# Stationary weights for the gate, up, key and query products of a two-layer hybrid decoder trunk

## The chip, the cores and the metric

The kernel runs on one core of one Trainium2 chip. The metric is the device time of one execution in microseconds (us), read as the median of the executions shown; lower is better.

## The reference

Sequence of 256 rows, width 1024, all float32. Two layers; each is a feed-forward network (FFN), a token mixer, and a second FFN, with RMS norms ahead of and behind each of them. The mixer of layer 0 is a gated causal convolution, that of layer 1 is causal attention with 8 heads. So there are four FFNs, numbered 0 to 3, with the convolution between 0 and 1 and the attention between 2 and 3.

```python
def rms_norm(x, g):
    y = x * lax.rsqrt(jnp.mean(x * x, axis=-1, keepdims=True) + RMS_EPS)
    return y * g

def swiglu_ffn(h, w_gate_up, w_down):          # 1024 -> 2 x 2816 -> 1024
    gate, up = jnp.split(h @ w_gate_up, 2, axis=-1)
    return (jax.nn.silu(gate) * up) @ w_down

for layer in range(2):
    f = swiglu_ffn(rms_norm(x, ffn_norm_pre[layer, 0]), ffn_w_gate_up[layer, 0], ffn_w_down[layer, 0])
    x = x + 0.5 * rms_norm(f, ffn_norm_post[layer, 0])
    h = rms_norm(x, mix_norm_pre[layer])
    y = conformer_conv(h, ...) if layer == 0 else attention(h, ...)   # attention: q, k, v, scores, softmax, values, w_o
    x = x + rms_norm(y, mix_norm_post[layer])
    f = swiglu_ffn(rms_norm(x, ffn_norm_pre[layer, 1]), ffn_w_gate_up[layer, 1], ffn_w_down[layer, 1])
    x = x + 0.5 * rms_norm(f, ffn_norm_post[layer, 1])
```

## The kernel before, in words

**Three products for one.** Every large product is made in fp32r from values split in two parts: `hi` is the value cast to fp32r by ScalarE (ACT), `lo` is what is left, value minus `hi`, by VectorE (DVE). A product is then hi·hi + hi·lo + lo·hi, three matmuls into one PSUM bank (`mm3` at L189 to L193, `rows_product` at L277 to L284).

**Weights.** `plan()` writes out the order in which 320 weight pieces of 128x1024 (512 KB) are used. SP's queue loads them in that order into four `raw` buffers (L155); `split_piece` (L158 to L179) makes `whi` on ACT and `wlo` on DVE, scaled by the norm's gain, into nine pairs of buffers (`wspl`). `use` keeps the order ten pieces ahead. A `raw` buffer is free when it is split, a `wspl` pair when the last matmul that reads it is done. A gate and up unit of an FFN has four pieces (each two of the eight contraction slices `k`, with 256 columns of gate and 256 of up), each down row block one.

**Activations.** `xT` holds the transposed rows, hi and lo, as two tiles of 8 slices x 256 columns. `turn(tt)` (L249 to L261) makes them for the rows of half `tt` (0 or 1): eight 128x128 PE transposes into two banks, then ACT's copy (L265) and DVE's difference (L266).

**An FFN** (`ffn`, L295) runs over 11 units of 256 hidden columns. For each unit and each half of the rows `gate_up(i, tt)` makes 24 matmuls with a slice of `xT` stationary and 512 weight columns moving, so the bank holds rows by [gate | up]; ACT applies silu (L310) and DVE multiplies (L311), both scaled by `rstds[tt]`, the reciprocal root of the pre norm, because the rows in `xT` were not normalised: in mode `"ffn"`, `pre_norm` (L228) hands the raw residual rows `xs` to `turn` and computes the reciprocal root beside it. `turn_act(i)` (L313) transposes the unit's activation by four PE transposes (L319) and splits it (L322, L323); `down` multiplies it with the down weights into four banks of accumulators. The first `FLEAD` units (1 for FFN 0, else 2) run half 0 of all of them before half 1, so that `turn(1)` can come later.

**The end of an FFN.** The down products of half 1 for the last 7 row blocks (`DEFER`) are kept for the end: `COVERED` of them run ahead of the last pair of half 0, then `after(0)` (post norm, residual, next pre norm, on ACT, DVE and POOL) starts, and the others run under it; `turn(0)` of the next stage stands ahead of the last two. `after(1)` follows the last one.

**Attention.** `kq(h)` makes the transposed keys and queries of a head in one bank of 2 x 256 columns, with the weights stationary and a part of `xT` (256 columns) moving: 24 matmuls each. Evicting them takes four instructions (L617 to L620). Then scores, softmax, transposed probabilities, values and output rows, with `kq` of the next head between a head's softmax and its probabilities.

**Order and PSUM.** The framework's scheduler orders each engine's instructions ahead of time by a priority (program order, raised by `tc.high_priority`) and by its own estimate of when an operand is ready; at run time each engine works in that order. Of the eight banks four are accumulators (tag `acc`), two are `mm` (products) and two `tr` (transposes, scores, spectra, values).

Of the kernel before, what the change touches and what calls it, by code (L numbers as in the profile page):

```python
# [20 lines left out]
F32 = mybir.dt.float32  # L21
F32R = mybir.dt.float32r
AF = mybir.ActivationFunctionType
# [28 lines left out]
COVERED = 1  # L52
# [45 lines left out]
def trunk(ctx, tc, x, wpk, gains, gcol, pvec, dft, wdw, bvec, out):  # L98
# [33 lines left out]
    pw = ps.tile([P, T], F32, name="pw", tag="mm")  # L132
# [56 lines left out]
    def mm3(out_ap, wh, wl, xh, xl, start, stop):  # L189

        nc.tensor.matmul(out_ap, wh, xh, start=start, stop=False)  # L191
        nc.tensor.matmul(out_ap, wh, xl, start=False, stop=False)  # L192
        nc.tensor.matmul(out_ap, wl, xh, start=False, stop=stop)  # L193
# [11 lines left out]
    def sumsq(src):  # L205
        junk = t2.tile([P, 512], F32, name="junk", tag="junk", bufs=2)
# [19 lines left out]
    rstds = {}  # L226

    def pre_norm(tt, pre):  # L228


        if pre == "ffn":
            normed[tt] = xs[:, tt, :].rearrange("p (h n) -> p h n", h=2)
        s = [sumsq(xs[:, tt, h * 512:(h + 1) * 512]) for h in range(2)]
        r, last = rstd_of(s[0], s[1], 1.0 / D, RMS_EPS)
        if pre == "ffn":
            rstds[tt] = r
            return last
        t = t4.tile([P, 2, 512], F32, name="xg", tag="t4")
        for h in range(2):
            xsl = xs[:, tt, h * 512:(h + 1) * 512]  # L240
            if pre is None:
                last = nc.vector.tensor_scalar(t[:, h, :], xsl, r, None, op0=ALU.mult)
            else:
                last = nc.vector.scalar_tensor_tensor(t[:, h, :], xsl, r, gain_t[pre][h],
                                                      op0=ALU.mult, op1=ALU.mult)
        normed[tt] = t
        return last

    def turn(tt, between=()):  # L249

        xg = normed.pop(tt)
        for h in range(2):
            p = ps.tile([P, 4, P], F32, name="ptr", tag="tr")
# [31 lines left out]

    def rows_unit(p, w, tt):

        for k in range(KD):
# [3 lines left out]
            mm3(p, xh, xl, wh[:, c], wl[:, c], k == 0, k == KD - 1)  # L292


    def ffn(f, after, *gains_used):  # L295
# [4 lines left out]
        def gate_up(i, tt):  # L300
# [5 lines left out]
            p = ps.tile([P, 2, 2 * P], F32, name="pgu", tag="mm")  # L306
            rows_unit(p.rearrange("p a b -> p (a b)"), w, tt)
            with tc.high_priority(offset=400):
                s = t2.tile([P, 2 * P], F32, name="sg", tag="sg", bufs=2)
                nc.scalar.activation(s, p[:, 0, :], AF.Silu, scale=rstds[tt])  # L310
                nc.vector.scalar_tensor_tensor(a[:, tt, :], p[:, 1, :], rstds[tt], s, op0=ALU.mult, op1=ALU.mult)  # L311

        def turn_act(i):  # L313

            a = raws.pop(i)[1]
            pt = ps.tile([P, 2, T], F32, name="pta", tag="tr")
# [29 lines left out]
        for i in range(FLEAD[f]):  # L346
            gate_up(i, 0)
        turn(1)
        for i in range(FLEAD[f]):
            gate_up(i, 1)  # L350
            if i:
                turn_act(i - 1)
        for i in range(FLEAD[f], NP):
# [6 lines left out]
            gate_up(i, 0)  # L360
            turn_act(i - 1)
            gate_up(i, 1)
# [31 lines left out]
    def conv_constants():  # L394
# [8 lines left out]
        for j in range(2):  # L403
            for h in range(2):
                p = ps.tile([NB, 512], F32, name="psp", tag="tr")
# [32 lines left out]
    def conv(after):  # L438
# [9 lines left out]
        def in_unit(q, tt):  # L448
# [5 lines left out]
            p = ps.tile([P, 2, 256], F32, name="pag", tag="mm")  # L454
# [15 lines left out]
        def filter_(h, tt):  # L470

            cols = slice(h * 512, (h + 1) * 512)
            with tc.high_priority(offset=300):
                U = []
                for j in range(2):
                    p = ps.tile([NB, 512], F32, name="pU", tag="tr")
# [20 lines left out]
        def layer_norm(tt):  # L497

            y = yacc[tt]
            with tc.high_priority(offset=300):  # L500
# [13 lines left out]
                for h in range(2):  # L514
                    p = ps.tile([P, 4, P], F32, name="pz", tag="tr")
# [40 lines left out]
    def attention(after):  # L556
# [45 lines left out]
        def kq(h):  # L602
# [4 lines left out]
            p = ps.tile([P, 2, T], F32, name="pkq", tag="mm")  # L607
            for s, n in enumerate("kq"):
                for k in range(KD):
                    wh, wl = pieces_kq[h2][n][k // 4]  # L610
                    o = (k % 4) * 256 + hj * P
                    mm3(p[:, s, :], wh[:, o:o + P], wl[:, o:o + P], xT[0][:, k, :], xT[1][:, k, :],
                        k == 0, k == KD - 1)
            with tc.high_priority(offset=400):
                kh = t2.tile([P, 2, T], F32R, name="kT", tag="t2")
                qh = t2.tile([P, 2, T], F32R, name="qT", tag="t2")
                nc.scalar.copy(kh[:, 0, :], p[:, 0, :])  # L617
                nc.vector.tensor_sub(kh[:, 1, :], p[:, 0, :], kh[:, 0, :].bitcast(F32))
                nc.scalar.activation(qh[:, 0, :], p[:, 1, :], AF.Copy, scale=sc)
                nc.vector.scalar_tensor_tensor(qh[:, 1, :], p[:, 1, :], sc, qh[:, 0, :].bitcast(F32),  # L620
# [3 lines left out]
        def scores(h):  # L624
            kh, qh = hd[h]["kq"]
            pS = ps.tile([P, NT, T], F32, name="pS", tag="tr")
# [27 lines left out]
        def probs(h):  # L654

            s = hd[h]["s"]
            pp = ps.tile([P, 3, P], F32, name="pp", tag="tr")
# [12 lines left out]
        def values(h):  # L670
            a = pT[h % 2]
            po = ps.tile([P, T], F32, name="po", tag="tr")
# [42 lines left out]
    pre_norm(0, "ffn")  # L715
    last = turn(0, between=first[:1])
    with tc.issue_after(last[0].ins):
        pre_norm(1, "ffn")
# [3 lines left out]
    conv(chain("mpost0", False, "ffn"))  # L722
    ctx2.close()
    ffn(1, chain("fpost1", True, "ffn"), "fpost1")
    ffn(2, chain("fpost2", True, None), "fpost2")
    ctx2 = ExitStack()
    attention(chain("mpost1", False, "ffn"))
# [94 lines left out]
```

## Time and profile before

| | us |
|---|---|
| median of 3 runs (975.83 to 980.27) | 977.95 |
| the profiled execution | 977.37 |
| its span, first to last instruction | 975.6 |

The profiled execution lies 0.06% under the median, and 1.8 us of its time lie outside the span. TensorE's matmuls (PE in the rows) are pipelined: the duration in a row runs past the start of the next one, so what a matmul costs in a dense stretch is the distance between two starts. PEld is the load of the stationary operand. In rows, `pgu` is the bank of a gate and up unit, `pta` that of the transposed activation, `ptr` that of `turn`, `pkq` keys and queries, `acc` the accumulators. Stages by time: FFN 0 to 204, convolution to 299, FFN 1 to 487, FFN 2 to 675, attention to 783, FFN 3 to the end.

### The profile page before, as it was taken

The page shows a single profiled execution, that of the slowest core. Times are in us where ns is not written, and L with a number is a line of the kernel's source. Part 1 is how long each engine was busy: PE and PEld are TensorE (multiplying, and loading weights), DVE is VectorE, ACT ScalarE, POOL GpSimd, SP SyncE. Part 2 cuts the span into 40 slices and gives each one's busy share as a digit, 9 for nine tenths or more (in the row PEclk, how much of TensorE's full clock was granted, in tenths as well). Part 3 has the DMA queues.
Part 4 walks back from the last instruction along what each step waited for, and adds up shares of the span by engine and source line. Part 5 has one row for each costly group of instructions (what it writes and reads, how often), then busy time and mean ns, then how long its engine had stood idle before and what let it go on. Part 6 is the DMA issues. An engine that isn't in the chain of part 4 may idle for free.

```text
span 975.6 us, 12708 instructions
## 1 busy us (share of the span) xinstructions
PE 958.1 (98%) x4514; PEld 786.8 (81%) x4514; DVE 618.6 (63%) x1064; ACT 550.8 (56%) x1029; POOL 22.1 (2%) x46
## 2 busy tenths in 40 slices
PE   8999999999999999999999999999999999999997
PEld 6887888876668888888888888887899888888885
DVE  5874565586667755655776565648887776564643
ACT  7764554472446745544765555546776676464541
POOL 1000000010011000000000000000000000000000
PEclk9999999999999999999999999999999999999999
DMA  7866464554326764645466464636643457555531
GB/s 262 297 232 203 130 220 148 190 198 151 108 65 198 261 192 154 228 156 194 160 202 227 156 224 154 212 134 215 195 154 127 131 165 247 171 192 196 170 111 43
DMA packets 48783, 174.93 MB, mean 179 GB/s; under 512 B 5673, under 2 KB 5673, under 8 KB 48720
## 3 DMA queue, kind: packets, MB, share of 16 engines
q1 hardware_dynamic: 48720, 174.13, 53.6%
q8 instruction: 35, 0.57, 0.2%
q14 instruction: 28, 0.23, 0.1%
HBM read 173.06 MB, written 1.05 MB: 178 GB/s over the span
## 4 chain that ended last, share of the span: by engine, by line
PE 93%; DVE 3%; ACT 1%; issue 1%; DMA 1%; POOL 0%; SPq 0%; DVEq 0%; POOLq 0%; ACTq 0%
PE pgu L191 16%; PE pgu L192 16%; PE pgu L193 16%; PE acc L283 10%; PE acc L282 10%; PE acc L284 10%; PE pta L319 2%; PE pkq L193 1%; PE pkq L192 1%; PE pkq L191 1%; PE pag L193 1%; PE pag L192 1%; PE pag L191 1%; DMA xs<-in_x_dram 1%; PE ptr L255 1%
## 5 line engine op out<-in xcount | busy, mean ns | idle before, releaser
L172 DVE SCALAR_TENSOR_TENSOR wlo<-raw,gc,whi 128x512 fp32r<-128x512 f32 x352 | 247.2, 748 | 92.3 <-ACT whi L171 89.1
L171 ACT ACTIVATE whi<-raw,gc 128x512 fp32r<-128x512 f32 x352 | 234.0, 717 | 98.5 <-PE acc L283 61.5
L191 PE MATMUL pgu<-whi,xTh 128*128 128x512 f32 x704 | 278.9, 396 | 0.8 <-ACT xTh L265 0.7
L192 PE MATMUL pgu<-wlo,xTh 128*128 128x512 f32 x704 | 275.1, 391 | 0.1
L193 PE MATMUL pgu<-whi,xTl 128*128 128x512 f32 x704 | 274.5, 391 | 0.0
L178 DVE TENSOR_TENSOR wlo<-raw,whi 128x512 fp32r<-128x512 f32 x240 | 155.4, 686 | 19.2 <-ACT whi L176 18.3
L176 ACT CAST whi<-raw 128x512 fp32r<-128x512 f32 x240 | 137.1, 619 | 44.5 <-PE pag L193 18.1
L191 PEld LDWEIGHTS pgu<-whi,xTh 128*128 128x128 f32 x704 | 132.6, 188 | 28.8 <-ACT xTh L265 1.4
L193 PEld LDWEIGHTS pgu<-whi,xTl 128*128 128x128 f32 x704 | 132.6, 188 | 27.9
L192 PEld LDWEIGHTS pgu<-wlo,xTh 128*128 128x128 f32 x704 | 132.7, 189 | 27.0 <-DVE wlo L172 0.5
L311 DVE SCALAR_TENSOR_TENSOR ar<-pgu,rr,sg 128x256 f32<-128x256 f32 x88 | 42.4, 482 | 163.6 <-ACT sg L310 163.5
L310 ACT ACTIVATE sg<-pgu,rr 128x256 f32<-128x256 f32 x88 | 41.7, 474 | 178.7 <-PE pgu L193 178.3
L282 PE MATMUL acc<-whi,ahi 128*128 128x512 f32 x352 | 137.5, 391 | 0.0
L283 PE MATMUL acc<-whi,alo 128*128 128x512 f32 x352 | 137.4, 390 | 0.0
L284 PE MATMUL acc<-wlo,ahi 128*128 128x512 f32 x352 | 137.1, 390 | 0.0
L283 PEld LDWEIGHTS acc<-whi,alo 128*128 128x128 f32 x352 | 66.1, 188 | 14.2 <-DVE alo L323 0.8
L284 PEld LDWEIGHTS acc<-wlo,ahi 128*128 128x128 f32 x352 | 66.1, 188 | 13.6
L282 PEld LDWEIGHTS acc<-whi,ahi 128*128 128x128 f32 x352 | 66.1, 188 | 13.6
L172 DVE SCALAR_TENSOR_TENSOR wlo<-raw,pv,whi 128x256 fp32r<-128x256 f32 (+1 forms) x72 | 37.3, 568 | 2.8 <-ACT whi L171 2.7
L171 ACT ACTIVATE whi<-raw,pv 128x256 fp32r<-128x256 f32 (+1 forms) x72 | 36.3, 573 | 3.7 <-PE acc L283 1.6
L191 PE MATMUL pkq<-xTh,whi 128*128 128x256 f32 x128 | 36.5, 285 | 0.0
L192 PE MATMUL pkq<-xTl,whi 128*128 128x256 f32 x128 | 36.5, 285 | 0.0
(126 smaller groups left out, 876.1 us busy)
## 6 DMA issues: line engine op xcount, KB each, us to landing
raw<-in_wpk_dram SPq DMA_DIRECT2D x320, 512.0 KB, 4.4
gain<-in_gains_dram SPq DMA_DIRECT2D x7, 512.0 KB, 4.3
xs<-in_x_dram SPq DMA_DIRECT2D x4, 256.0 KB, 6.5
out_dram<-xs SPq DMA_DIRECT2D x4, 256.0 KB
dm<-in_dft_dram SPq DMA_DIRECT2D x1, 368.0 KB
taps<-in_wdw_dram SPq DMA_DIRECT2D x1, 124.0 KB
braw<-in_bvec_dram SPq DMA_DIRECT2D x6, 4.0 KB
ys<-in_bvec_dram SPq DMA_DIRECT2D x2, 2.0 KB
```

The lines of the kernel that those rows point to most:

```text
L171: nc.scalar.activation(hi[:, o:o + n], raw[:, o:o + n], AF.Copy, scale=g)
L172: nc.vector.scalar_tensor_tensor(lo[:, o:o + n], raw[:, o:o + n], g, hb[:, o:o + n], op0=ALU.mult, op1=ALU.subtract)
L176: nc.scalar.copy(hi[:, o:o + 512], raw[:, o:o + 512])
L178: eng.tensor_sub(lo[:, o:o + 512], raw[:, o:o + 512], hb[:, o:o + 512])
L191: nc.tensor.matmul(out_ap, wh, xh, start=start, stop=False)
L192: nc.tensor.matmul(out_ap, wh, xl, start=False, stop=False)
L193: nc.tensor.matmul(out_ap, wl, xh, start=False, stop=stop)
L282: nc.tensor.matmul(o, xh, wh[:, cols], start=first, stop=False)
L283: nc.tensor.matmul(o, xl, wh[:, cols], start=False, stop=False)
L284: nc.tensor.matmul(o, xh, wl[:, cols], start=False, stop=last)
L310: nc.scalar.activation(s, p[:, 0, :], AF.Silu, scale=rstds[tt])
L311: nc.vector.scalar_tensor_tensor(a[:, tt, :], p[:, 1, :], rstds[tt], s, op0=ALU.mult, op1=ALU.mult)
```

## The change

Four edits, with the constants `COVERED` from 1 to 2 and the new `FTURN` of 5.

1. `xT` becomes one tile of 8 slices x [hi 256 | lo 256], so that 512 moving columns take both parts. `both_parts` makes a product with a 128x128 block of weights stationary: per slice one matmul of `whi` with 512 columns (hi·hi lands in the left half of a bank, hi·lo in the right half) and one of `wlo` with the 256 hi columns, into the left half. `joined` sums the halves when the bank is read: ACT copies the right half to SBUF, DVE adds the left one.
2. Gate and up of all units from `FLEAD` on (10 in FFN 0, 9 in each of the others) are made that way, gate and up of 128 hidden columns each in a bank of its own. Their result is transposed already: `turn_act` stays for the first `FLEAD` units only. Keys and queries take the same form.
3. The mode `"ffn"` of the pre norm goes: the rows are multiplied by the reciprocal root before `turn`, at the start of every FFN, as it was done ahead of the attention. `gate_up_rows` (the first units) loses the scale.
4. The tags `mm` and `tr` become one of four banks. In FFN 0, `turn(1)` may issue only after the sixth slice (`FTURN`) of the first unit. `junk` has one buffer instead of two.

```diff
-COVERED = 1
+COVERED = 2
+FTURN = 5
...
     def pre_norm(tt, pre):
-        if pre == "ffn":
-            normed[tt] = xs[:, tt, :].rearrange("p (h n) -> p h n", h=2)
         s = [sumsq(xs[:, tt, h * 512:(h + 1) * 512]) for h in range(2)]
-        r, last = rstd_of(s[0], s[1], 1.0 / D, RMS_EPS)
-        if pre == "ffn":
-            rstds[tt] = r
-            return last
+        r, _ = rstd_of(s[0], s[1], 1.0 / D, RMS_EPS)
...
-        return (const.tile([P, KD, T], F32R, name="xTh"), const.tile([P, KD, T], F32R, name="xTl"))
-    xT = new_xT()
+        return const.tile([P, KD, 2, T], F32R, name="xT")
+    x2 = new_xT()
+    xT = [x2[:, :, j, :] for j in range(2)]
...
+    def both_parts(p, w, cols):
+        flat = p.rearrange("p a b -> p (a b)")
+        def high(k):
+            nc.tensor.matmul(flat, w(k)[0][:, cols(k)], x2[:, k, :, :].rearrange("p a b -> p (a b)"),
+                             start=k == 0, stop=k == KD - 1)
+        for k in range(KD):
+            if k < KD - 1:
+                high(k)
+            nc.tensor.matmul(p[:, 0, :], w(k)[1][:, cols(k)], x2[:, k, 0, :], start=False, stop=False)
+        high(KD - 1)
+    def joined(out_, p):
+        nc.scalar.copy(out_, p[:, 1, :])
+        nc.vector.tensor_add(out_, p[:, 0, :], out_)
...
+        def gate_up(i):
+            w = [use(("gu", f, i, q)) for q in range(KD // 2)]
+            for j in range(2):
+                pg, pu = (ps.tile([P, 2, T], F32, name=n, tag="mm", bufs=4) for n in ("pg", "pu"))
+                for s, p in enumerate((pg, pu)):
+                    def cols(k, o=s * 256 + j * P):
+                        return slice((k % 2) * 512 + o, (k % 2) * 512 + o + P)
+                    both_parts(p, lambda k: w[k // 2], cols)
+                with tc.high_priority(offset=400):
+                    g = t2.tile([P, T], F32, name="sg", tag="sg", bufs=2)
+                    joined(g, pg)
+                    nc.scalar.activation(g, g, AF.Silu)
+                    a = t2.tile([P, T], F32, name="af", tag="af", bufs=2)
+                    joined(a, pu)
+                    nc.vector.tensor_mul(a, a, g)
+                    hl = t2.tile([P, 2, T], F32R, name="act", tag="t2")
+                    nc.scalar.copy(hl[:, 0, :], a)
+                    nc.vector.tensor_sub(hl[:, 1, :], a, hl[:, 0, :].bitcast(F32))
+                act[2 * i + j] = (hl[:, 0, :], hl[:, 1, :])
...
         for i in range(FLEAD[f]):
-            gate_up(i, 0)
-        turn(1)
+            done = gate_up_rows(i, 0)
+        with tc.issue_after(done[FTURN].ins) if f == 0 else nullcontext():
+            turn(1)
...
-            gate_up(i, 0)
-            turn_act(i - 1)
-            gate_up(i, 1)
+            gate_up(i)
             if i == FLEAD[f]:
+                turn_act(i - 1)
                 for j in range(i - 1):
                     down_pair(j, range(NT))
             down_pair(i - 1, range(NT))
-        turn_act(NP - 1)
...
-            p = ps.tile([P, 2, T], F32, name="pkq", tag="mm")
-            for s, n in enumerate("kq"):
-                for k in range(KD):
-                    wh, wl = pieces_kq[h2][n][k // 4]
-                    o = (k % 4) * 256 + hj * P
-                    mm3(p[:, s, :], wh[:, o:o + P], wl[:, o:o + P], xT[0][:, k, :], xT[1][:, k, :],
-                        k == 0, k == KD - 1)
+            pk, pq = (ps.tile([P, 2, T], F32, name=n, tag="mm", bufs=4) for n in ("pk", "pq"))
+            for p, n in ((pk, "k"), (pq, "q")):
+                w = pieces_kq[h2][n]
+                both_parts(p, lambda k: w[k // 4], lambda k: slice((k % 4) * 256 + hj * P, (k % 4) * 256 + hj * P + P))
...
+                joined(ks, pk)
+                nc.scalar.copy(kh[:, 0, :], ks)
+                nc.vector.tensor_sub(kh[:, 1, :], ks, kh[:, 0, :].bitcast(F32))
+                joined(qs, pq)
```

## Rows read from the trace of the kernel before

**Rows 1.** The page: busy time of the engines; shares of the chain that ended last, by line.
```profile
PE 958.1 (98%) x4514; PEld 786.8 (81%) x4514; DVE 618.6 (63%) x1064; ACT 550.8 (56%) x1029; POOL 22.1 (2%) x46
...
PE pgu L191 16%; PE pgu L192 16%; PE pgu L193 16%; PE acc L283 10%; PE acc L282 10%; PE acc L284 10%; PE pta L319 2%; PE pkq L193 1%; PE pkq L192 1%; PE pkq L191 1%; PE pag L193 1%; PE pag L192 1%; PE pag L191 1%; DMA xs<-in_x_dram 1%; PE ptr L255 1%
```
**Rows 2.** Busy us (count) of PE, PEld, DVE, ACT, POOL, then PEclk; unit, attention.
```profile
367.69:384.48 16.79, 16.79 (x77) 13.91 (x76) 9.74 (x15) 9.03 (x15) 0.00 (x0) 1.00 0.60 190
...
700.00:764.00 64.00, 63.77 (x500) 61.31 (x500) 52.47 (x129) 44.00 (x119) 0.00 (x0) 1.00 0.50 158
```
**Rows 3.** Timeline of PE around one activation transpose and in a gate product.
```profile
367.69 0.60 PE L319 MATMUL pta<-ident,ar 128*128 128x128 f32 x4
...
368.36 0.39 PE L192 MATMUL pgu<-wlo,xTh 128*128 128x512 f32 x1
...
370.88 0.39 PE L191 MATMUL pgu<-whi,xTh 128*128 128x512 f32 x1
371.11 0.39 PE L192 MATMUL pgu<-wlo,xTh 128*128 128x512 f32 x1
```
**Rows 4.** Timeline of PE in a key product.
```profile
715.29 0.28 PE L191 MATMUL pkq<-xTh,whi 128*128 128x256 f32 x1
715.41 0.28 PE L192 MATMUL pkq<-xTl,whi 128*128 128x256 f32 x1
```
**Rows 5.** Groups by line and form: evictions on ACT and DVE.
```profile
L310 ACT ACTIVATE sg<-pgu,rr 128x256 f32<-128x256 f32 x88 | 41.7, 474 | 178.7 <-PE pgu L193 178.3
...
L322 ACT CAST ahi<-pta 128x512 fp32r<-128x512 f32 x44 | 25.8, 586 | 7.4 <-PE pta L319 7.4
...
L617 ACT CAST kT<-pkq 128x256 fp32r<-128x256 f32 x8 | 2.8, 355 | 2.9 <-PE pkq L193 2.9
...
L323 DVE TENSOR_TENSOR alo<-pta,ahi 128x512 fp32r<-128x512 f32 x44 | 30.4, 691 | 8.7 <-ACT ahi L322 6.4
...
L618 DVE TENSOR_TENSOR kT<-pkq,kT 128x256 fp32r<-128x256 f32 x8 | 3.3, 417 | 1.9 <-ACT kT L617 1.9
```
**Rows 6.** Timeline, FFN 2 to attention: the norms of half 0.
```profile
664.30 0.60 ACT L208 ACTIVATE junk<-acc 128x512 f32<-128x512 f32 x1 [1.20 <-PE acc L284]
...
671.51 0.88 DVE L242 TENSOR_SCALAR xg<-xs,rr 128x512 f32<-128x512 f32 x2 [0.73 <-POOL rr L202]
...
672.14 1.06 PE L255 MATMUL ptr<-ident,xg 128*128 128x128 f32 x8 [0.84 <-DVE xg L242]
```
**Rows 7.** Timeline, FFN 1 to FFN 2: `turn(0)`, the norms of half 1, `turn(1)`.
```profile
483.07 1.04 PE L255 MATMUL ptr<-ident,xs 128*128 128x128 f32 x8
...
487.01 0.58 ACT L208 ACTIVATE junk<-acc 128x512 f32<-128x512 f32 x1
...
497.60 1.03 PE L255 MATMUL ptr<-ident,xs 128*128 128x128 f32 x8
...
498.87 0.50 PE L191 MATMUL pgu<-whi,xTh 128*128 128x512 f32 x1 [0.24 <-ACT xTh L265]
```
**Rows 8.** Timeline, FFN 0 to the convolution: `turn(0)` and `turn(1)`.
```profile
200.71 0.63 PE L255 MATMUL ptr<-ident,xg 128*128 128x128 f32 x4 [0.77 <-DVE xg L244]
...
210.55 1.29 PE L255 MATMUL ptr<-ident,xg 128*128 128x128 f32 x8 [1.01 <-DVE xg L244]
```
**Rows 9.** Timeline of the first 15 us.
```profile
5.86 1.04 PE L255 MATMUL ptr<-ident,xs 128*128 128x128 f32 x8
...
6.07 0.55 POOL L202 TENSOR_TENSOR rr<-rb,nhalf 128x1 f32<-128x1 f32 x1 [4.77 <-DVE rb L200]
...
9.65 0.52 PE L255 MATMUL ptr<-ident,xs 128*128 128x128 f32 x3 [2.76 <-DMA xs<-in_x_dram]
...
12.75 5.01 ACT L171 ACTIVATE whi<-raw,gc 128x512 fp32r<-128x512 f32 x8
```
**Rows 10.** Busy time as in rows 2, PEclk behind POOL: behind FFN 0's spectra; the start.
```profile
93.20:96.20 3.00, 3.00 (x7) 2.39 (x8) 0.00 (x0) 0.58 (x1) 0.00 (x0) 0.50 0.36 134
6.60:9.65 3.05, 0.30 (x3) 0.09 (x2) 2.52 (x4) 2.31 (x4) 0.02 (x1) 1.00 0.95 366
```

More of the change, by code (lines that the diff above doesn't have):

```diff
@@ L131, in trunk @@
     nc.vector.memset(idle, 0.0)
-    pw = ps.tile([P, T], F32, name="pw", tag="mm")
+    pw = ps.tile([P, T], F32, name="pw", tag="mm", bufs=4)
     for _ in range(WARM):
@@ L192, in mm3 @@
         nc.tensor.matmul(out_ap, wh, xl, start=False, stop=False)
-        nc.tensor.matmul(out_ap, wl, xh, start=False, stop=stop)
+        return nc.tensor.matmul(out_ap, wl, xh, start=False, stop=stop)
     def rstd_of(s0, s1, scale, eps):
@@ L252, in turn @@
         for h in range(2):
-            p = ps.tile([P, 4, P], F32, name="ptr", tag="tr")
+            p = ps.tile([P, 4, P], F32, name="ptr", tag="mm", bufs=4)
             for j in range(4):
@@ L284, in rows_product @@
             nc.tensor.matmul(o, xh, wl[:, cols], start=False, stop=last)
+    def both_parts(p, w, cols):
[11 more added lines that the diff above has]
+        nc.vector.tensor_add(out_, p[:, 0, :], out_)
     def rows_unit(p, w, tt):
+        done = []
         for k in range(KD):
@@ L291, in rows_unit @@
             xh, xl = (xT[j][:, k, tt * P:(tt + 1) * P] for j in range(2))
-            mm3(p, xh, xl, wh[:, c], wl[:, c], k == 0, k == KD - 1)
+            done.append(mm3(p, xh, xl, wh[:, c], wl[:, c], k == 0, k == KD - 1))
+        return done
     def ffn(f, after, *gains_used):
@@ L298, in ffn, with gate_up_rows @@
         raws = {}
-        def gate_up(i, tt):
+        def gate_up_rows(i, tt):
             if i not in raws:
@@ L305, in gate_up @@
             w, a = raws[i]
-            p = ps.tile([P, 2, 2 * P], F32, name="pgu", tag="mm")
-            rows_unit(p.rearrange("p a b -> p (a b)"), w, tt)
+            p = ps.tile([P, 2, 2 * P], F32, name="pgr", tag="mm", bufs=4)
+            done = rows_unit(p.rearrange("p a b -> p (a b)"), w, tt)
             with tc.high_priority(offset=400):
                 s = t2.tile([P, 2 * P], F32, name="sg", tag="sg", bufs=2)
-                nc.scalar.activation(s, p[:, 0, :], AF.Silu, scale=rstds[tt])
-                nc.vector.scalar_tensor_tensor(a[:, tt, :], p[:, 1, :], rstds[tt], s, op0=ALU.mult, op1=ALU.mult)
+                nc.scalar.activation(s, p[:, 0, :], AF.Silu)
+                nc.vector.tensor_mul(a[:, tt, :], s, p[:, 1, :])
+            return done
         def turn_act(i):
             a = raws.pop(i)[1]
-            pt = ps.tile([P, 2, T], F32, name="pta", tag="tr")
+            pt = ps.tile([P, 2, T], F32, name="pta", tag="mm", bufs=4)
             for tt in range(NT):
@@ L616, in kq @@
                 qh = t2.tile([P, 2, T], F32R, name="qT", tag="t2")
[L617 to L620, printed above, removed]
+                ks = t2.tile([P, T], F32, name="sg", tag="sg", bufs=2)
+                joined(ks, pk)
+                nc.scalar.copy(kh[:, 0, :], ks)
+                nc.vector.tensor_sub(kh[:, 1, :], ks, kh[:, 0, :].bitcast(F32))
+                qs = t2.tile([P, T], F32, name="af", tag="af", bufs=2)
+                joined(qs, pq)
+                nc.scalar.activation(qh[:, 0, :], qs, AF.Copy, scale=sc)
+                nc.vector.scalar_tensor_tensor(qh[:, 1, :], qs, sc, qh[:, 0, :].bitcast(F32),
                                                op0=ALU.mult, op1=ALU.subtract)
@@ L671, in values @@
             a = pT[h % 2]
-            po = ps.tile([P, T], F32, name="po", tag="tr")
+            po = ps.tile([P, T], F32, name="po", tag="mm", bufs=4)
             for kt in range(NT):
@@ L714, in trunk @@
     first += [load_piece() for _ in range(2)]
-    pre_norm(0, "ffn")
+    pre_norm(0, None)
     last = turn(0, between=first[:1])
     with tc.issue_after(last[0].ins):
-        pre_norm(1, "ffn")
+        pre_norm(1, None)
         for split_first in first[1:]:
@@ L721, in trunk @@
     ffn(0, chain("fpost0", True, "mpre0"), "fpost0", "mpre0")
-    conv(chain("mpost0", False, "ffn"))
+    conv(chain("mpost0", False, None))
     ctx2.close()
-    ffn(1, chain("fpost1", True, "ffn"), "fpost1")
+    ffn(1, chain("fpost1", True, None), "fpost1")
     ffn(2, chain("fpost2", True, None), "fpost2")
     ctx2 = ExitStack()
-    attention(chain("mpost1", False, "ffn"))
+    attention(chain("mpost1", False, None))
     ctx2.close()
```

17 lines of the change are left out of this document (8 added, 9 removed).

## The prediction

> **What bounds the kernel now.** I read the page first, then stretches, then single matmuls. On the page PE is busy 98% of the span and the chain that ended last is nearly all PE lines [rows 1]: gate and up 48%, down and the other row products 30%, the activation's transposes 2%. In the stretches DVE and ACT have room in an FFN: of a unit of 16.79 us they fill 9.74 and 9.03 us; in the attention DVE fills 52.47 of 64 us, 82%, at a PE that is full [rows 2]. So a PE instruction taken out of a dense stretch gives its whole step back, and the question is what the removed work was covering. Steps are read between starts, not from durations: a 512-column matmul of a gate product steps 0.227 us (0.39 in its row), and four transposes between two such matmuls add 0.67 - 0.227 = 0.44 us [rows 3]. A 256-column matmul, each with a stationary load of its own, steps 0.120 us [rows 4]. A unit checks this: 72 x 0.227 + 0.44 = 16.8 us.
>
> **The change, term by term.** The sum goes against the profiled execution, 977.37 us (0.58 under the median).
>
> *Transposes.* Of 44 units 37 lose `turn_act`; 7 keep it. 37 x 0.44 = **-16.3 us**, all on the path, as the chain runs through them [rows 1, 3].
>
> *Narrower matmuls.* A unit had 48 matmuls of 512 columns. It gets 32 of 512 and 32 of 256: the same 24,576 columns, in 16 instructions more. 32 x (0.227 + 0.120) - 48 x 0.227 = 0.21 us, 37 times: **+7.8 us** [rows 3, 4]. Both steps lie about 13 ns above columns over 2.4 GHz, so this is the price of an instruction, and I take it as additive when the widths alternate; a wider load cost isn't to be expected, since 256 columns with weights stationary already run at 0.120 [rows 4].
>
> *Keys and queries.* The same form takes instructions out here: per head 48 of 256 columns become 16 of 512 and 16 of 256, 5.55 for 5.76 us; 8 heads: **-1.7 us** [rows 3, 4].
>
> *Evictions in the FFN.* Per unit ACT goes from two silus and a 512 copy (1.53 us) to eight 256-column operations (six at 0.36, two at 0.47: 3.1 us); DVE has eight at about 0.42 instead of two at about 0.48 and one at 0.69, 3.3 for 1.7 us [rows 5]. A unit then fills 11.4 us of DVE and 10.6 of ACT in 16.6 [rows 2]: 0. What hides it: a bank is written once a unit for 2.8 us, and has some 13 us to be read. What is late next: all four pieces of a unit come free only in its last product (2.8 us), so the splits for the next unit crowd behind it; but five of nine pairs are already split, and the sixth is wanted 9 us after it comes free. SP's queue keeps its order and 6 loads a unit; they bunch by the same few us.
>
> *Start of the four FFNs, half 0.* The reciprocal root and the scale now stand ahead of the transposes. The path from the first sum of squares to the transposes is 7.84 us where that form exists already [rows 6]. Under it run the matmuls after half 0's first bank is done. That was 3 + 36, 8.85 us less the 0.2 us to the first sum; with `COVERED` = 2 one row block (6 matmuls) moves ahead of it: 3 + 30, 7.3 us. So the transposes wait about 0.5 us, and behind them nothing covers the split of `xT`, some 0.3 (0.24 at `turn(1)` [rows 7]; taken a bit higher, as hi and lo are both awaited). FFN 1 to FFN 2 and attention to FFN 3 had no wait (the first in [rows 7]): +0.7 each. FFN 2 to attention waited 0.84 already and has the smaller cover: +0.2 [rows 6]. Convolution to FFN 1 has 50 matmuls of cover: 0. FFN 0 to the convolution waits twice, 0.77 and 1.01 [rows 8]; half 1's wait shrinks by what half 0's transposes move behind its last down product: -0.7. Together **+0.9 us**; bounds -1 (only that last gain) and +5 (each of four waits a whole row block, 1.36 us, longer).
>
> *Half 1* costs nothing: 10.6 us from its first sum to its transposes, set by two units' matmuls, against a path of 7.84 [rows 6, 7]. The earlier row block also covers the last unit's act, made by some six short evictions (about 3.5 us) under 30 matmuls (6.8 us): 0.
>
> *Start of the kernel.* The first transposes now wait for the reciprocal root, ready at 6.62, and a scale of 0.44: 7.2 instead of 5.86 [rows 6, 9]; splits and first matmuls follow 1.3 us later. Against that PE no longer stands until 9.65 for half 1 of x, and ACT reaches the next three pieces about 1 us before 12.75, as half 1's two copies come later [rows 9]. But the old order filled the gaps with half 1's matmuls, which now come after the sixth slice. `turn(1)` moves its 8 transposes, 2 copies and 2 differences, no DMA; it queues nothing behind it on PE but that unit. I take **+0.9 us**, between -1 (the standing time given back) and +2.5 (the idle time in front of 9.65 paid again).
>
> *Attention.* Two copies on ACT (0.36) and two sums on DVE (0.42) per head join the split of keys and queries [rows 5]; DVE goes to about 58 of 63 us, 92% [rows 2]. PE fills the longer way to the scores with the next head's product, which finds a bank in the common four. Between 0 and 6.7 us (16 sums wholly on the path) I take **+1.0**, nearer to the bottom since PE is full there now.
>
> Sum: -16.3 + 7.8 - 1.7 + 0.9 + 0.9 + 1.0 = -7.4, so 977.4 - 7.4 = **970.0 us**, 0.8% under the median. One stretch may also change by luck: behind the filter spectra of FFN 0 the clock is granted at 0.50, the level of 1.2 GHz, and seven matmuls take 3.00 us, 0.43 each, against 1.00 or 2.4 GHz in the other stretches [rows 2, 10]; without it 8 x 0.2 = 1.6 us would go.
>
> **The rivals.**
> *Evictions hold PE (slower).* Place: the end of each of 37 units, where splits that wait for a pair stand in ACT's and DVE's order ahead of evictions, and DVE's difference for the next unit's fourth piece, wanted 2 us into its first product instead of 4, comes late. It decides from 0.33 us of waiting per unit (7.4 + 4.9 over 37). At 0.5 us: 970 + 18.5 = **988.5**. Against it: DVE at 69% [rows 2].
> *DVE becomes the bound in attention.* The whole 6.7 us instead of 1.0: **975.7**. For it 82% now [rows 2], against it PE's order has spare matmuls.
> *The pre norm is not covered.* Each of the four changed starts and the attention's wait a row block longer than I count, 5 x 1.36: **976.8**. For it the 0.84 that already waits [rows 6].
> *The clock falls at the new waits.* Around four waiting `turn(0)`s PE does little but transposes for 2 us; a stretch like that behind the spectra [rows 10] costs 1.6 each time: **976.4**. Against it: nearly 3 us of waiting at the start, three transposes in it, leave the clock at 1.00 [rows 10].
> *The price of an instruction goes away* when wide and narrow matmuls alternate, so that only columns count: the term of 7.8 us falls to nothing, **962.2**. Against it stand both steps, 13 ns above their columns [rows 3, 4]. The Trainium skill (TensorE: Matmul & The Clock Gate, Back-to-back issue gap) has a rule of this kind: columns over 2.4 GHz and 2.5 ns more for an isolated warm matmul, which makes that term an estimate of 1.5 us. By that rule the steps would be 0.216 and 0.109 us; the trace has 0.227 and 0.120 and disagrees in both widths.
>
> **How the numbers follow.** This kernel's measurement can tell about 0.5% (4.9 us) from no change: faster is below 973.1. Forecast 0.60; price gone 0.03; DVE in attention 0.13; norm uncovered 0.10; clock 0.04; evictions 0.10. Faster 0.63, same 0.27, slower 0.10. The range reaches down to 964, where the low bounds of waits and start (-1.9 each), the attention's and the clock's 1.6 lead together, short of the rival at 962.2, and up to 979, past the three middle cases; the slower rival stays out.
>
> **What would show it.** Right: 148 fewer `pta` transposes; alternating steps of 0.227 and 0.120 us in a gate product; units of 16.5 to 16.6 us; DVE 68 to 70% of a unit; waits of 0.5 to 1 us at the `turn(0)` of FFN 2, the attention and FFN 3. Wrong: units above 16.8 us, an alternating pair above 0.36 us, idle time of PE ahead of `pS` or `pp`, waits of 2 us at a `turn`, or a granted clock of 0.50 in a new place.

## The result and the profile after

The changed kernel takes 995.49 us (median of 4 runs, 993.82 to 995.69), the kernel before 978.63 beside it: 1.0184 times, 95% interval 1.017 to 1.0198. It is 1.8% slower where 0.8% faster was forecast. Its profiled execution, the shortest of the four, took 993.82 us, 992.0 of them span, 16.4 more than before.

The first gate or product matmul of each stage divides the span, and shows at once that the loss does not lie in the FFN units:

| stage (us) | before | after | difference |
|---|---|---|---|
| start and FFN 0 | 203.48 | 207.81 | +4.3 |
| convolution | 96.10 | 100.95 | +4.9 |
| FFN 1 | 187.13 | 187.37 | +0.2 |
| FFN 2 | 188.19 | 188.13 | -0.1 |
| v product of the attention | 22.66 | 23.66 | +1.0 |
| attention, from the first key product to FFN 3 | 85.17 | 91.26 | +6.1 |
| FFN 3 to the end | 192.87 | 192.87 | 0.0 |

The page of the kernel after: busy time, and the chain by line. These answer to [rows 1].

```profile
PE 960.9 (97%) x4830; PEld 796.8 (80%) x4830; DVE 684.0 (69%) x1281; ACT 596.1 (60%) x1230; POOL 22.4 (2%) x46
...
PE pu L287 14%; PE pg L287 13%; PE acc L278 10%; PE acc L277 10%; PE acc L279 10%; PE pu L293 7%; PE pg L293 7%; PE pgr L194 2%; PE pgr L192 2%; PE pgr L193 2%; PE pk L287 1%; DVE wlo L173 1%; PE pag L192 1%; PE pag L193 1%; PE pag L194 1%
```

`pta` is no longer among the lines of the chain that the page shows: 28 of its 176 transposes are left. PE is busy 2.8 us more than before, in a span 16.4 us longer: most of the loss is standing time. What it stood for is in the list of PE's waits (engine, line, what was waited for: us in total, times, longest), first of the kernel before, then of the kernel after:

```profile
PE ptr L255 <- DMA xs<-in_x_dram: 2.8, 1, 2.8
...
PE ptr L255 <- DVE xg L244: 1.8, 2, 1.0
PE pU L481 <- DVE u L466: 1.5, 1, 1.5
```

```profile
PE pS L192 <- ACT qT L658: 5.9, 4, 2.3
PE pgr L193 <- DVE wlo L173: 3.4, 2, 3.0
PE pU L519 <- DVE u L504: 2.8, 3, 0.9
PE ptr L249 <- DVE xg L236: 2.6, 4, 0.9
PE ptr L249 <- DVE xg L238: 2.1, 2, 1.3
PE y L532 <- DVE ys L526: 1.9, 1, 1.9
```

The scores wait for the queries, four times; the convolution's spectra wait three times instead of once, and its output once where it did not; a new wait of 3.0 us stands at the start. The single wait of 2.8 us for x is gone.

Stretches of the kernel after (as [rows 2, 10]): an FFN unit, the attention, 3.1 us of the start, 6 us of the convolution.

```profile
559.79:576.51 16.72, 16.72 (x89) 14.31 (x88) 11.15 (x21) 10.38 (x21) 0.00 (x0) 1.00 0.57 193
708.00:786.00 78.00, 72.05 (x421) 61.49 (x420) 64.46 (x157) 54.93 (x149) 0.00 (x0) 1.00 0.47 148
...
16.90:20.00 3.10, 3.10 (x9) 2.34 (x8) 3.10 (x6) 1.44 (x2) 0.00 (x0) 0.50 0.72 223
...
280.00:283.00 3.00, 3.00 (x5) 1.37 (x5) 1.23 (x3) 0.00 (x0) 0.00 (x0) 0.50 0.48 172
283.00:286.00 3.00, 3.00 (x8) 2.14 (x7) 2.27 (x7) 0.00 (x0) 0.55 (x1) 0.50 0.01 3
```

The unit has a full PE and took 16.72 us, with DVE at 67%. In the attention PE stands 78.00 - 72.05 = 5.95 us, about the whole of that stage's loss. The last three rows have the clock at 0.50, the level of 1.2 GHz, in two places where it was 1.00 before; each lies behind a wait of PE (3.0 us for `wlo`, 1.9 us for `ys`).

The timeline of PE in a gate product of the kernel after, which answers to [rows 3, 4]:

```profile
561.19 0.40 PE L287 MATMUL pg<-xT,whi 128*128 128x512 f32 x1
561.42 0.28 PE L293 MATMUL pg<-xT,wlo 128*128 128x256 f32 x1
561.54 0.40 PE L287 MATMUL pg<-xT,whi 128*128 128x512 f32 x1
561.78 0.28 PE L293 MATMUL pg<-xT,wlo 128*128 128x256 f32 x1
561.90 0.40 PE L287 MATMUL pg<-xT,whi 128*128 128x512 f32 x1
```

Two pairs take 561.90 - 561.19 = 0.71 us. Over the kernel the mean step is 0.236 us from a wide to a narrow matmul and 0.117 back, 0.353 for the pair where 0.347 was forecast.

### The profile page after: what moved, and what is told of

It reads as the page before. It is cut to its first block, busy times and chain, and to the rows that moved or that the text cites. A ratio compares the mean times of both kernels' runs of the same rounds, so it can differ in the third digit from the quotient of the medians.

```text
span 992.0 us, 13714 instructions
## 1 busy us (share of the span) xinstructions
PE 960.9 (97%) x4830; PEld 796.8 (80%) x4830; DVE 684.0 (69%) x1281; ACT 596.1 (60%) x1230; POOL 22.4 (2%) x46
## 4 chain that ended last, share of the span: by engine, by line
PE 89%; DVE 4%; ACT 3%; issue 2%; DMA 1%; POOL 1%; DVEq 0%; POOLq 0%; SPq 0%; ACTq 0%
PE pu L287 14%; PE pg L287 13%; PE acc L278 10%; PE acc L277 10%; PE acc L279 10%; PE pu L293 7%; PE pg L293 7%; PE pgr L194 2%; PE pgr L192 2%; PE pgr L193 2%; PE pk L287 1%; DVE wlo L173 1%; PE pag L192 1%; PE pag L193 1%; PE pag L194 1%
## 5 line engine op out<-in xcount | busy, mean ns | idle before, releaser
L287 PE MATMUL pg<-xT,whi 128*128 128x512 f32 x592 | 215.6, 398 | 0.0
L287 PE MATMUL pu<-xT,whi 128*128 128x512 f32 x592 | 215.1, 397 | 0.0
L293 PE MATMUL pu<-xT,wlo 128*128 128x256 f32 x592 | 154.2, 281 | 0.0
L293 PE MATMUL pg<-xT,wlo 128*128 128x256 f32 x592 | 154.0, 281 | 0.0
L278 PE MATMUL acc<-whi,act 128*128 128x512 f32 x328 | 128.1, 391 | 0.0
L277 PE MATMUL acc<-whi,act 128*128 128x512 f32 x328 | 128.0, 391 | 0.0
L279 PE MATMUL acc<-wlo,act 128*128 128x512 f32 x328 | 127.9, 390 | 0.0
L287 PEld LDWEIGHTS pu<-xT,whi 128*128 128x128 f32 x592 | 111.6, 189 | 19.9
L293 PEld LDWEIGHTS pu<-xT,wlo 128*128 128x128 f32 x592 | 111.8, 189 | 6.9
L293 PEld LDWEIGHTS pg<-xT,wlo 128*128 128x128 f32 x592 | 111.7, 189 | 6.5
L278 PEld LDWEIGHTS acc<-whi,act 128*128 128x128 f32 x328 | 61.6, 188 | 12.8 <-DVE act L719 0.2
L277 PEld LDWEIGHTS acc<-whi,act 128*128 128x128 f32 x328 | 61.5, 188 | 11.4 <-ACT act L718 0.2
```

The costliest lines, as they stand in the source:

```text
L277: nc.tensor.matmul(o, xh, wh[:, cols], start=first, stop=False)
L278: nc.tensor.matmul(o, xl, wh[:, cols], start=False, stop=False)
L279: nc.tensor.matmul(o, xh, wl[:, cols], start=False, stop=last)
L287: nc.tensor.matmul(flat, w(k)[0][:, cols(k)], x2[:, k, :, :].rearrange("p a b -> p (a b)"), start=k == 0, stop=k == KD - 1)
L293: nc.tensor.matmul(p[:, 0, :], w(k)[1][:, cols(k)], x2[:, k, 0, :], start=False, stop=False)
```

## The experiments

Three parts were suspects: the common tag of four banks (edit 4), the alternation of widths (edit 1), and the norm ahead of the transposes (edit 3). "Before" is the kernel before on the same chip, 977.04 us in the first four runs, 977.6 in the next four, 977.48 in the last two.

### Wide matmuls first, then narrow ones

```diff
+        for k in range(KD - 1):
+            high(k)
         for k in range(KD):
-            if k < KD - 1:
-                high(k)
             nc.tensor.matmul(p[:, 0, :], w(k)[1]...)
```

(the eighth wide one stays last)

> The changed kernel with one edit: a product issues its wide matmuls of slices 0 to 6 first, then its eight narrow ones, then the last wide one, so that the width changes twice in a product and not sixteen times. Theory 1, the change of width costs: a wide and a narrow matmul in turn step 0.353 us where 0.227 + 0.120 = 0.347 was forecast; in runs of one width the steps go back to 0.227 and 0.120, a unit's four products from 11.27 to about 11.1 us, and the whole to about 990 us (5 to 6 less than 995.5). Theory 2, the extra time comes from reading the weights or writing half a bank, whatever the order: steps and time stay, 994 to 996.

991.16 us, 1.0141 (1.0116 to 1.0166). The timeline of its PE in one product:

```profile
560.50 1.77 PE L287 MATMUL pu<-xT,whi 128*128 128x512 f32 x7
562.11 1.11 PE L293 MATMUL pu<-xT,wlo 128*128 128x256 f32 x8
563.07 0.40 PE L287 MATMUL pu<-xT,whi 128*128 128x512 f32 x1
563.30 1.77 PE L287 MATMUL pg<-xT,whi 128*128 128x512 f32 x7
```

Seven wide ones step (562.11 - 560.50)/7 = 0.230 us, eight narrow ones 0.120. A unit takes 16.61 us, its four products 11.15 where the alternating order takes 11.27. The same work in another order gives 0.11 us a unit, 4 us in 37, and the ratio is 0.43% (4.2 us) under that of the kernel after. So the alternating order costs some 4 us. The two profiled spans differ by 1.8 us only: this one has 0.50 for 3.4 us of its attention, which takes 1.1 us longer, and waits 1.2 us more ahead of its transposes.

### The common tag alone, in the kernel before

```diff
-            p = ps.tile([P, 2, T], F32, name="pkq", tag="mm")
+            p = ps.tile([P, 2, T], F32, name="pkq", tag="mm", bufs=4)
-            pS = ps.tile([P, NT, T], F32, name="pS", tag="tr")
+            pS = ps.tile([P, NT, T], F32, name="pS", tag="mm", bufs=4)
...
```

(and so for every other tile of the two tags)

> The kernel before with one edit: its tags mm and tr become one tag of four banks, as in the changed kernel. Theory 1, the common banks take away the work that filled the waits: the next head's key product no longer stands ahead of the scores, PE waits 1 to 2 us per head for the evicted query, attention grows by 5 to 8 us, the convolution by 2 to 5, whole 986 to 991. Theory 2, the longer evictions of the new products are to blame: attention and convolution stay as before, 977 to 980.

985.0 us, 1.0074 (1.0052 to 1.0095). Its waits of PE:

```profile
PE pS L191 <- ACT qT L619: 5.9, 4, 1.9
PE pU L481 <- DVE u L466: 2.8, 3, 0.9
...
PE y L494 <- DVE ys L488: 1.9, 1, 1.9
```

The same three totals, to a tenth, without any stationary weights, `joined` or moved norm. The attention loses 6.1 us and the convolution 2.5. FFN 0 ends 0.2 us earlier than before, but by luck: the tag costs 1.4 us at its start (a wait of 2.0 us for `whi` is new), and 1.6 come back behind the spectra, where the clock is 1.00 here and 0.50 in [rows 10].

### Keys and queries in banks of their own

```diff
-            pk, pq = (ps.tile([P, 2, T], F32, name=n, tag="mm", bufs=4) for n in ("pk", "pq"))
+            pk, pq = (ps.tile([P, 2, T], F32, name=n, tag="acc" if h < H - 1 else "mm", bufs=4) for n in ("pk", "pq"))
```

(The accumulators of the attention are taken later, when the last head's product has begun.)

> The changed kernel with one edit: keys and queries of the first seven heads use the accumulators' four banks, which stand idle until the output rows begin. Theory 1 (common banks): the next head's key product fills the wait for the scores again, attention loses 5 to 7 us, whole 989 to 991. Theory 2 (longer evictions, ACT and DVE in order): the waits ahead of the scores stay above 1 us per head, whole 994 to 996.

987.3 us, 1.0101 (1.008 to 1.0122). The attention takes 84.3 us, 7.0 less than in the kernel after and 0.9 less than before. The four waits of `pS` come from the common tag, not from the longer eviction.

### Memsets of the convolution's constants later

```diff
+        with tc.issue_after(later):
             nc.gpsimd.memset(braw, 0.0)
```

> The changed kernel with one edit: POOL's four memsets for the convolution's biases wait until half 1's first transposes are split. Theory 1, POOL and DVE get in each other's way in SBUF: DVE's scale of half 1 (two instructions that take 2.56 us beside the memsets, 0.88 elsewhere) takes 0.9 us, PE's wait of 2.99 us at 16.3 shrinks to 1.2 to 1.5, the clock stays at 1.00 in the first 25 us, whole 991.5 to 993. Theory 2, the scale is slow for another reason or other work comes last there: the wait stays, 994.5 to 996.5.

993.57 us, 1.0164 (1.0146 to 1.0182). The edit did not move the memsets: on the chip POOL still ran them at the same time (13.06 us, after 12.98), and the scale of half 1 took 2.70 us. The run says nothing on the suspicion.

### Two tags again, in the changed kernel

```diff
-                pg, pu = (ps.tile([P, 2, T], F32, name=n, tag="mm", bufs=4) for n in ("pg", "pu"))
+                pg, pu = (ps.tile([P, 2, T], F32, name=n, tag=g) for n, g in (("pg", "mm"), ("pu", "tr")))
-            pS = ps.tile([P, NT, T], F32, name="pS", tag="mm", bufs=4)
+            pS = ps.tile([P, NT, T], F32, name="pS", tag="tr")
...
```

(products in `mm`, transposes, scores, spectra and values in `tr`, two banks each)

> The changed kernel with one edit: two banks tagged mm and two tagged tr again, the gate bank of a unit and keys and queries from mm, the up bank and all transposes, scores, spectra and values from tr. Theory 1, the common tag is what the attention and most of the convolution lose by: the key product of the next head stands ahead of the scores again, attention loses 6 to 7 us, convolution 2 to 3, units stay at 16.72, whole 985.5 to 988. Theory 2, the convolution's loss comes from the clock that falls to 0.50 there and not from the banks: convolution keeps its 4.9 us more, whole 988.5 to 990.

985.86 us, 1.0078 (1.0051 to 1.0104). The timeline of PE between a head's queries and its scores, first in the kernel after, then here:

```profile
713.32 0.39 PE L287 MATMUL pq<-xT,whi 128*128 128x512 f32 x1
715.08 0.38 PE L192 MATMUL pS<-kT,qT 128*128 128x256 f32 x1 [1.37 <-ACT qT L658]
715.30 0.28 PE L193 MATMUL pS<-kT,qT 128*128 128x256 f32 x1
715.42 0.39 PE L287 MATMUL pk<-xT,whi 128*128 128x512 f32 x1
```

```profile
713.26 0.40 PE L287 MATMUL pq<-xT,whi 128*128 128x512 f32 x1
713.50 0.40 PE L287 MATMUL pk<-xT,whi 128*128 128x512 f32 x1
713.73 0.28 PE L293 MATMUL pk<-xT,wlo 128*128 128x256 f32 x1
...
714.79 0.28 PE L293 MATMUL pk<-xT,wlo 128*128 128x256 f32 x1
715.03 0.39 PE L192 MATMUL pS<-kT,qT 128*128 128x256 f32 x1
```

With the tag shared, PE's order has nothing between the last query matmul and the scores. With tags of their own, eight matmuls of the next head's keys stand there, and the scores start as early without a wait. The attention takes 84.2 us, the convolution 96.3, as before. Where the FFN 0 of the kernel after lost 4.3 us, this one loses 8.9, with the clock at half in two stretches of 6.8 us: 0.9 of the 4.6 more lie at the start and 3.7 behind the spectra, where the kernel after had 1.00. So the gain is larger in the two stages (11.7 us) than in the sum.

This stretch of its attention shows what DVE does when nothing else holds PE:

```profile
708.00:778.00 70.00, 69.91 (x417) 60.84 (x416) 63.47 (x157) 55.34 (x149) 0.00 (x0) 1.00 0.49 170
```

DVE is at 91%, and PE is full.

### Memsets on DVE

```diff
-            nc.gpsimd.memset(braw, 0.0)
+            nc.vector.memset(braw, 0.0)
```

(the other constants of the convolution too)

> The changed kernel with one edit: the memsets for the convolution's biases are DVE's instead of POOL's, so that POOL writes nothing to SBUF beside the scale of half 1. Theory 1, POOL's memsets slow that scale: its two instructions take 0.9 instead of 2.56 us, PE's wait of 2.99 us ahead of 16.3 shrinks by 1.5 to 1.8, and if the clock then stays at 1.00 another 1.6 us goes: whole 991.5 to 994. Theory 2, the scale is slow because of DMA traffic into SBUF at the start: it stays above 2 us, whole 994.5 to 996.

996.18 us, 1.0185 (1.0158 to 1.0213). Timeline rows of POOL, DVE and PE in the kernel after, then the scale and two later waits of PE in this one:

```profile
12.98 1.84 POOL L460 MEMSET braw<- 128x1024 f32 x2
13.07 2.56 DVE L236 TENSOR_SCALAR xg<-xs,rr 128x512 f32<-128x512 f32 x2 [0.67 <-POOL rr L203]
...
16.33 0.50 PE L193 MATMUL pgr<-wlo,xT 128*128 128x512 f32 x1 [2.99 <-DVE wlo L173]
```

```profile
13.07 0.88 DVE L236 TENSOR_SCALAR xg<-xs,rr 128x512 f32<-128x512 f32 x2 [0.67 <-POOL rr L203]
...
14.67 0.50 PE L193 MATMUL pgr<-wlo,xT 128*128 128x512 f32 x1 [0.63 <-DVE wlo L173]
...
43.27 1.19 PE L277 MATMUL acc<-whi,ahi 128*128 128x512 f32 x4 [2.03 <-ACT ahi L339]
```

The scale loses 1.68 us beside the memsets, and without them the wait of 2.99 us shrinks to 0.63. Of that only 1.0 us comes through, as PE now waits 2.03 us at 43 for the first activation (0.52 in the kernel after). The first matmul of the filter spectra and a stretch behind them, in the kernel after, then here:

```profile
96.57 0.65 PE L445 MATMUL psp<-taps,dm 31*80 31x512 f32 x1
...
99.80:103.20 3.40, 3.40 (x18) 2.70 (x18) 0.00 (x0) 0.77 (x2) 0.00 (x0) 1.00 0.80 298
```

```profile
95.56 0.65 PE L445 MATMUL psp<-taps,dm 31*80 31x512 f32 x1
...
99.80:103.20 3.40, 3.40 (x12) 2.88 (x11) 0.00 (x0) 0.38 (x1) 0.00 (x0) 0.50 0.58 216
```

So this run is 1.0 us ahead until the spectra, and FFN 0 ends later all the same (208.30) because the clock fell behind them. The first theory is right on the scale and wrong on the time.

### Two tags, and one covered row block

```diff
-COVERED = 2
+COVERED = 1
```

(beside the two tags)

> The kernel with its own tags again (run beside this one) with COVERED back at 1, so that one row block more of down products runs under the norms of half 0. Theory 1, the waits ahead of turn(0) at the four ends of an FFN are the price of the normalised rows and shrink with a longer cover: 0.5 to 1.2 us less at the ends of FFN 0, 1 and 2, whole 1.5 to 3 us below its neighbour. Theory 2, the last unit's activation then comes late: PE waits for act ahead of the last pair of down products of half 0, by 1 us or more in each FFN, whole the same or 2 to 4 us above its neighbour.

983.18 us, 1.0054 (1.0037 to 1.0071); the interval overlaps that of its neighbour, so the stages decide. PE at the start of FFN 2 in the kernel after, and here:

```profile
494.76 1.06 PE L249 MATMUL ptr<-ident,xg 128*128 128x128 f32 x8 [0.82 <-DVE xg L236]
...
497.59 0.50 PE L194 MATMUL pgr<-whi,xT 128*128 128x512 f32 x1 [0.33 <-DVE xT L260]
```

```profile
492.83 1.06 PE L249 MATMUL ptr<-ident,xg 128*128 128x128 f32 x8 [0.83 <-DVE xg L236]
```

The transposes wait as long with either value. What differs is the work behind them: from the first transpose to the first gate matmul it is 1.37 us, with two down matmuls, in the kernel after, and 2.75 us, with eight, here, and eight hide the split of `xT`. FFN 2 gets 0.7 us shorter and the v product 1.0.

### The norm ahead of the transposes alone, in the kernel before

```diff
-    pre_norm(0, "ffn")
+    pre_norm(0, None)
...
-    attention(chain("mpost1", False, "ffn"))
+    attention(chain("mpost1", False, None))
```

(likewise at the other starts; silu and the gate's product lose their scale)

> The kernel before with one edit: the rows are multiplied by the reciprocal root ahead of turn in every FFN, and the gate's eviction has no scale (edit 3 of the change alone, COVERED 1, no order put on turn(1)). Theory 1, the norm ahead of the transposes costs what was forecast, 0.7 us at two starts, nothing at a third and 1 to 2.5 us at the first: 978.5 to 981. Theory 2, the first start alone loses 4 us or more, since half 1's scale stands between the splits of the first weights: 981.5 to 984.

983.65 us, 1.005 (1.0032 to 1.0068). Of 6.6 us of span, 4.6 lie in FFN 0 (208.08 against 203.48), 1.1 in FFN 1 and 0.5 in the attention. The scale takes 2.56 us here as well. The first down matmul of FFN 0's second unit shows where the 4.6 us arise, in the kernel before, here, and in the kernel after:

```profile
50.38 0.39 PE L282 MATMUL acc<-whi,ahi 128*128 128x512 f32 x1
```

```profile
53.38 0.39 PE L277 MATMUL acc<-whi,ahi 128*128 128x512 f32 x1
```

```profile
57.58 0.40 PE L277 MATMUL acc<-whi,act 128*128 128x512 f32 x1
```

The start costs 3.0 us. The other 1.6 come behind the spectra, where the clock is at 0.50 for 6.8 us here and for 3.4 in the kernel before. So the second theory has the whole time right, but not its 4 us or more at the start.

### Two tags, one covered block, wide matmuls first

The edits of three runs above in one.

> The changed kernel with the two tag pairs of before (two banks mm, two tr, up products and transposes in tr), COVERED at 1, and in each product of both parts first the eight wide matmuls, then the eight narrow ones. Theory (the losses are three and add up: the common tag, the alternation of widths, the norm ahead of the transposes): own tags and COVERED gave 983.2, and the order of widths gave 0.11 us in a unit with the common tag, 37 x 0.11 = 4.1 us: 979.0, units of 16.60 us, an attention of 84 us. Rival (what own tags and the order of widths give is the same stalls at a bank, counted twice): 982 to 983, units of 16.70. Rival (the wide run's faster units came only with the clock's luck in that run): units of 16.72 and 983.

980.05 us (10 runs), 1.0027 (1.0016 to 1.0038). Units of 16.61 us, FFN 1 at 186.4, FFN 2 at 186.5, attention at 84.3: the stages add up as the first theory says, and both rivals, with units of 16.70 and 16.72, fall. In the time the order gave some 2.6 us of the 4.1 expected. FFN 0 still ends at 211.84.

### The same, with FFN 0 as before

```diff
-    pre_norm(0, None)
+    pre_norm(0, "ffn")
...
-            gate_up(i)
+            if f == 0:
+                gate_up_rows(i, 0)
+                turn_act(i - 1)
+                gate_up_rows(i, 1)
+            else:
+                gate_up(i)
```

(beside the edits of the run above; likewise for half 1, and `turn(1)` loses its order behind `FTURN`)

> The same, and FFN 0 as in the kernel before: raw rows transposed, the reciprocal root applied behind the gate and up products, the rows form with its activation transposes for all eleven units. Theory (the start of the kernel loses 4 us or more because norm and scale stand ahead of the first transposes, and ten stationary units give back only 10 x 0.19 = 1.9 us): FFN 0 ends at 203.5 us as before, the rest as own_tags_wide_first, with FFN 1 at 186.6, FFN 2 at 187, attention 84 and FFN 3 at 192: a span of 971.9, a time of 973.7, 0.4% under before. Rival (what FFN 0 loses is not its start but its end, the norm ahead of the convolution): FFN 0 ends at 206 or later, 976. Rival (the lost time moves: later stages start with other splits ahead): FFN 1 or the attention over 1 us longer than in own_tags_wide_first, 975 or more.

973.25 us, 0.9955 (0.9942 to 0.9968): faster than both kernels, and 0.45 us from the expected sum. From its page, the same two parts, and then one unit:

```profile
PE 951.9 (98%) x4710; PEld 790.6 (81%) x4710; DVE 661.7 (68%) x1227; ACT 583.9 (60%) x1180; POOL 22.0 (2%) x46
...
PE pu L293 10%; PE pg L293 10%; PE acc L284 10%; PE acc L283 10%; PE acc L285 10%; PE pgr L192 7%; PE pgr L194 6%; PE pgr L193 6%; PE pu L299 5%; PE pg L299 5%; PE pq L293 2%; PE pk L293 2%; PE pag L194 1%; PE pag L192 1%; PE pag L193 1%
```

```profile
559.23:575.84 16.61, 16.61 (x89) 14.34 (x88) 10.95 (x22) 10.14 (x22) 0.00 (x0) 1.00 0.57 190
```

PE's busy share is back at 98%, with 6.2 us less of work than before. FFN 0 ends at 202.80 and FFN 1, FFN 2 and the attention keep 186.4, 186.5 and 84.2 us. In this setting the stationary form of FFN 0, with the norm it needs at the start, costs 9.0 us of span and 6.8 of the medians; ten units cannot pay that at 0.19 us each. Of the 9.0 us 8.7 lie at the start, with the clock at 0.50 for 10.2 us there in the run above and 1.00 in this one, and 2.2 behind the spectra, where 6.8 us at 0.50 stand against 3.4; the units give back 1.8. The run undoes norm, form and the order of `turn(1)` together, so it doesn't tell what each of them costs.

## Why the prediction was wrong

The forecast said -7.4 us, the trace has +16.4. Of the 23.8 us between them 6.1 lie in the attention, 5.7 in FFN 0, 5.6 in the convolution and 6.5 in FFN 1 to 3 with the v product, most of these in the units. The step that failed first is the sentence "PE fills the longer way to the scores with the next head's product, which finds a bank in the common four". It counted banks and not the order in which they are given out. In the program the scores of a head come ahead of the next head's keys. With one tag for both, PE's order kept them so; with two tags the keys could stand ahead. That the framework hands out the buffers of one tag in program order is my reading of these two orders, and no run looked into the framework itself. That the tag is the cause is shown, by adding it alone (+6.1 us in the attention), by undoing it (-7.1), and by undoing it for keys and queries only (-7.0). The rival of DVE in the attention had nearly the same price (6.7 us instead of 1.0), but the sums that it blames are not in the tag-only run, and the loss is. Of the forecast's signs of being wrong two came: idle time ahead of `pS`, and a clock of 0.50 in new places. The clock's rival, too, had the wrong place: it looked at the four `turn(0)`s.

*Convolution.* Edit 4 changed the tags of `pag`, `pU` and `pz` too, and the working gave them no term at all. Measured +4.9 us: the tag alone gives 2.5, waits at `pU` and `y`. The rest goes with the clock, at 0.50 for over 6 us behind them: with the same tag there the stage lost 2.5 and 2.7 us in two runs whose clock stayed at 1.00 (the tag alone; keys and queries in banks of their own), 3.5 in one with 3.4 us at 0.50 (memsets on DVE), and with two tags nothing. Why the clock fell in some of these and not in others stays open.

*Transposes*, -16.3: right. 28 `pta` transposes are left of 176; 24 of them still lie on the chain, six groups of 0.44 us.

*Narrower matmuls*, +7.8: mis-sized. The steps do not add when the widths alternate: products of 11.27 us instead of 11.10, units of 16.72 instead of 16.56. The gain of 37 units is 37 x (16.80 - 16.72) = 3.0 us, not 8.5. The sign that the forecast had set for a failure, a pair above 0.36, was too coarse: some 5 ns a pair take most of the gain in 37 x 32 pairs. With the widths grouped the products take 11.15 us, so about 4 of the 5 ns come back.

*Price of an instruction goes away*: fell. The pair would be 0.320 us by columns alone and took 0.353. By the Trainium skill (TensorE: Matmul & The Clock Gate, Back-to-back issue gap), which gives columns over 2.4 GHz plus 2.5 ns for an isolated warm matmul, it would be 0.325, an estimate; the trace, a stream of loads and matmuls, lies 28 ns above it.

*Evictions in the FFN*, 0: right. DVE fills 67% of a unit and PE waits for nothing; the rival with slower evictions falls, although it was the only one that had the sign.

*Start of the kernel*, +0.9 with bounds -1 and +2.5: mis-sized and out of its bounds. FFN 0 ends 4.3 us late, where 10 x -0.23 + 0.9 should have made it end 1.4 early. The start itself costs 7.2 us (57.58 against 50.38); the luck behind the spectra came, with a clock of 1.00, and gives back 1.7, and the units give 1.1. The first transposes came when forecast, at 7.32 us (the forecast has 7.2, where its own 6.62 and 0.44 give 7.06). What was not seen comes behind them: half 1's scale ahead of the next weight splits on DVE, priced at 0.44 us each [rows 6] without what POOL does at that moment (1.0 us comes back with the memsets off POOL), and a clock of 0.50 behind the wait. The norm alone costs 3.0 us at the start. The common tag alone costs 1.4 there, but two tags in the changed kernel do not give it back (58.43). What makes up the rest of the 7.2 stays open: no run takes the order of `turn(1)` (`FTURN`) or the one buffer of `junk` out by itself.

*Starts of the other FFNs*: +0.7 each was somewhat small (waits of 0.82 and 0.33 at FFN 2, 0.69 and 0.31 at FFN 3). The -0.7 at the convolution did not come: its transposes wait 0.78 and 1.33 us where [rows 8] have 0.77 and 1.01. The reason given for the waits was wrong: `COVERED` left the wait of the transposes as it was and took away down matmuls that hid the split behind them. At the attention that made +1.0 where +0.2 was forecast.

*Keys and queries, DVE in the attention*: near once the tag is out of the way. DVE at 91% (92% forecast) left PE full, and the stage, FFN 3's start in it, came out 1.0 us shorter than before (forecast: 0.0). No run takes its three terms apart.

The failure lies in the parts that the forecast gave the least room: waits were bounded one by one, by rows of the old order, while one edit changed the order itself.

## What to carry to other kernels

A buffer tag is part of the schedule: before merging two, list what each use of the one may no longer overtake in the other. When a change needs a preparation at the head of each stage, price it separately for the first stage, where nothing covers it, and leave that stage in the old form if its gain doesn't pay. Group matmuls of one width where the order is free.

## What the runs showed of the hardware

Alternating 512 and 256 columns, the narrow ones into half of the same bank, costs 3 to 6 ns a pair over the steps of each width in a row (0.353 against 0.230 + 0.120 and 0.227 + 0.120 us). No run tells the width from the half bank.

Two DVE scales of 128x512 take 0.88 us together in a quiet stretch [rows 6]. They took 2.56 us while POOL cleared two tiles, and 0.88 again without that. The list of this tile's instructions in the kernel after (min, median and max ns of one) gives 2.03 us for the longer of the two:

```profile
L236 DVE TENSOR_SCALAR xg<-xs,rr x2: 606/1318/2031, 13.1 to 15.0; 128x512 f32<-128x512 f32 x2
```

The Trainium skill (SBUF — State Buffer, Who interferes with whom) says that `tensor_scalar` can enter a mode that needs the port pair that DVE shares with GpSimd, and that whoever comes second is blocked until the other is done; the trace agrees in the main, as the first scale, which started at 13.07, 0.09 us behind the memsets, ended at 15.10, after both (14.82). The 0.28 us left behind them are less than the 0.44 that [rows 6] give for one, so it did not stand still for all of their time. No run shows the opposite order.

The granted clock stood at 0.50 behind several new waits of PE (16.90 to 20.00, 280 to 286), and at 1.00 behind others, the four of the scores among them. In two runs with the same four waits (wide matmuls first, and memsets on DVE) it stood at 0.50 for 3.4 us of the attention. So a wait of this size does not settle the clock by itself.
